# Input projections of a two-layer diffusion step: one store for both halves of a result, three buffers for latent keys and values, and the first modulation in columns of 256

## The chip, the core and the metric

The kernel runs on one core of one Trainium2 chip. The metric is device time in microseconds (us), the median of several executions. PE is the matmul engine (PEld its weight loads), DVE the vector engine, ACT the scalar engine, POOL GpSimd, SP the sync engine, whose queue issues nearly all DMAs here.

## What is computed

Two layers, each a token mixer (three groups of attention heads) and a gated convolutional feed-forward part, on 128 context tokens and 1024 latent tokens. Each token is scaled and shifted by six modulation vectors per layer, which come from two conditioning vectors. Cut to what matters here:

```python
mods = jax.nn.silu(cond) @ w_ada + b_ada
sh_m, sc_m, gt_m, sh_f, sc_f, gt_f = [m[:, None, :] for m in jnp.split(mods, 6, axis=-1)]
h = rms_norm(x, g_pre_mix) * (1 + sc_m) + sh_m
q_na, k_na, v_na, q_mla, ckv, k_rope, q_g, k_g, v_g = mixer_projections(
    h, w_in, mla_g_q, mla_w_uq, mla_g_kv, gqa_g_q, gqa_g_k)
...
o = jnp.concatenate([o_na, o_mla, o_gqa], axis=-1) @ w_out
x = x + gt_m * rms_norm(o, g_post_mix)
h = rms_norm(x, g_pre_ffn) * (1 + sc_f) + sh_f
x = x + gt_f * rms_norm(conv_ffn(h, ffn_w_up, ffn_conv_w, ffn_conv_b, ffn_w_down), g_post_ffn)
```

D_MODEL is 1024, so `w_ada` is 1024 x 6144 for each layer. The parts gt_m, sh_f and sc_f (2, 3 and 4) are first needed after the attention.

## The kernel before

The tokens are nine tiles of 128. Every layer runs in stages: `phase_a` (input projections), `phase_b` (attention), `phase_c` (output projection), `phase_u` (up projection, convolution, gate) and `Down`. Matrix products keep 32-bit accuracy by splitting each operand in a high and a low half and adding three products, so results that are read again are stored as two halves, `hi` and `lo`. `evac2` makes them from a PSUM bank: ACT writes `hi`, then DVE writes `lo = src - hi` (L205 and L206, or L208 and L209 with a scale).

`phase_a` first projects the values (V part: L374 to L376, 512 wide), then the latent heads (MLA: `mla_tile`, 416 wide, nine tiles), then the grouped heads (GQA: `gqa_tile`, nine tiles, with the pieces `mla_k` and `mla_v` spread between them), then the neighbourhood heads (NA: six groups `m` of 128 columns, L591, three chunks of 384 tokens in three PSUM banks, 72 matmuls for each group). Results go to DRAM tensors (QT, QM, KT, KM, VT, VM) by DMAs on SP's queue and are loaded again by `phase_b`. `ev` tiles hold latent keys and values on their way out, in two buffers. In the trace's names the buffers `ev2` of the NA groups also read `ev`, since trailing numbers are left out there.

Layer 0 makes its modulations 2, 3 and 4 beside this, on DVE: `ada_dve` (L297 to L324) is a generator. For each part and each stretch of `wd` columns it loads eight tiles `wadv` of 128 x `wd` (L305, two buffers) and multiplies and adds each into two accumulators `aacc`, one for each conditioning vector (L308 for the first tile, L311 for the other seven). Then PE transposes the accumulators (L320), and DVE sums the transposes (L321). It yields after each load's two instructions, and once more before the transposes: nine steps for a stretch. With `wd` = 512 there are 3 x 2 stretches, 48 loads and 54 steps.

`phase_a` advances that generator 9 + 4 times in the MLA loop, 18 times in the GQA loop and four times in each of six NA groups: 55 times in all. After the products of the last NA group, what is left of it is run to its end:

```python
if g0 and mi == 1:
    for g in ag:
        finish(g, [])
for c in range(NCH):
    sb = p.tile([128, 2, CN], F32R, name="ev2", bufs=3)
```

In layer 1 no generator runs in `phase_a`; its modulations are made in `phase_u` of layer 0 by the same function with 512 columns.

Instructions are recorded in the order in which the code makes them, and a scheduler then orders each engine's list. Each engine runs its list in order. A DMA that waits for its data or its buffer holds everything behind it on SP's queue. The first instruction of the attention on PE is a score matmul of the first latent head (L679, tile SA). The functions that the change touches:

Of the kernel before, what the change touches and what calls it, by code (L numbers as in the profile page):

```python
# [14 lines left out]
F32 = mybir.dt.float32  # L15
F32R = mybir.dt.float32r
# [15 lines left out]
CN = 384  # L32
# [13 lines left out]
def tile_kernel(ctx: ExitStack, tc: tile.TileContext, I, O):  # L46
    nc = tc.nc
# [15 lines left out]
    QT = [dram.tile([2, 12 * 64, NT], F32, name=f"QT{l}") for l in range(L)]  # L63
# [296 lines left out]
    def kcols(t):  # L360
        return (0 if t == 0 else 128) + t * 128

    def phase_a(l, z, H, w, before, rest):
# [35 lines left out]
        adst, adp = right("ad")  # L399
        ag = [ada_dve(l, z, adp, (2, 3, 4), 512)] if l == 0 else []  # L400
# [16 lines left out]
        def mla_tile(t):  # L417
# [35 lines left out]
            krT = [p.tile([32, 128], F32R, name=f"krT{e}", bufs=2) for e in range(2)]  # L453
            evac2(krT[0], krT[1], tp[0:32, 384:512])
            for e in range(2):
                nc.sync.dma_start(out=KM[l][e, :, 64:96, kc:kc + 128].rearrange("h p n -> p h n"),
                                  in_=krT[e].bitcast(F32).unsqueeze(1).to_broadcast([32, 4, 128]))
# [16 lines left out]
            qT = [p.tile([128, 4, 128], F32R, name=f"qT{e}", bufs=2) for e in range(2)]  # L474
            evac2(qT[0][0:96], qT[1][0:96], tq[0:96, :].rearrange("p (h n) -> p h n", h=4), 96.0 ** -0.5)
            for e in range(2):
                nc.sync.dma_start(out=QM[l][e, :, :, t * 128:(t + 1) * 128].rearrange("h p n -> p h n"),
                                  in_=qT[e][0:96].bitcast(F32))

        def gqa_tile(w, t):  # L480
# [22 lines left out]
            gT = [p.tile([128, 4, 128], F32R, name=f"qT{e}", bufs=2) for e in range(2)]  # L503
            evac2(gT[0], gT[1], tp.rearrange("p (h n) -> p h n", h=4))
            for e in range(2):
                nc.sync.dma_start(
                    out=QT[l][e, 384:768, t * 128:(t + 1) * 128].rearrange("(a p) n -> p a n", p=128),
                    in_=gT[e][:, 0:3].bitcast(F32))
                nc.sync.dma_start(out=KT[l][e, 384:512, kcols(t):kcols(t) + 128],
                                  in_=gT[e][:, 3].bitcast(F32))  # L510

        def mla_k(c0, n):
            for j in range(2):
# [5 lines left out]
                ks = p.tile([128, 2, 512], F32R, name="ev", bufs=2)  # L519
                evac2(ks[:, 0, :n], ks[:, 1, :n], kp[:, :n])  # L520
                for e in range(2):
                    for q in range(2):
                        nc.sync.dma_start(out=KM[l][e, 2 * j + q, 0:64, cs],
                                          in_=ks[q * 64:(q + 1) * 64, e, :n].bitcast(F32))

        def mla_v(t):
# [4 lines left out]
            vs = p.tile([128, 4, 128], F32R, name="ev", bufs=2)  # L531
# [29 lines left out]
        with tc.tile_pool(reuse_waits="tile", name="an", bufs=1) as p:  # L561
# [19 lines left out]
            for g0, ms in ((0, (0, 1, 2, 3)), (512, (4, 5))):  # L581
                whi, wlo = weights(l, wp, G_NA[0] + g0, len(ms) * 128)
                for mi, m in enumerate(ms):
# [13 lines left out]
                    for c in range(NCH):  # L597
# [3 lines left out]
                        for e in range(2):  # L601
                            sf = sb[:, e].bitcast(F32)
                            if m < 3:
                                nc.sync.dma_start(
                                    out=QT[l][e, m * 128:(m + 1) * 128, c * CN:(c + 1) * CN], in_=sf)
                            else:
                                kt = KT[l][e, (m - 3) * 128:(m - 2) * 128]
                                if c == 0:
                                    nc.sync.dma_start(out=kt[:, 0:128], in_=sf[:, 0:128])
                                    nc.sync.dma_start(out=kt[:, 256:128 + CN], in_=sf[:, 128:CN])  # L610
                                else:
                                    nc.sync.dma_start(
                                        out=kt[:, 128 + c * CN:128 + (c + 1) * CN], in_=sf)
# [804 lines left out]
```

## Time and profile before

| | |
|---|---|
| median of 3 runs | 3363.74 us (3360.38 to 3366.98) |
| the profiled execution's own time | 3362.17 us |
| its span | 3360.4 us |
| PE busy | 3205.2 us, 95% |
| DVE busy | 2169.4 us, 65% |
| ACT busy | 1544.0 us, 46% |
| POOL busy | 1124.0 us, 33% |

The span is the time from the first to the last instruction; 1.8 us of the execution's own time lie outside it. A busy time counts the engine's instructions; whether idle time of an engine costs anything is read from what waited. In the views of waits, `A <- B` says that A started when B was done. A timeline row gives start and duration in us and, in brackets, how long the engine was idle before and what ended that.

### The profile page before, as it was taken

How to read it: one execution, taken by the hardware profiler on the slowest of the kernel's cores; microseconds unless marked ns; L12 is line 12 of the kernel's file. 1: busy time of each engine (PE TensorE's matmuls, PEld its weight loads, DVE VectorE, ACT ScalarE, POOL GpSimd, SP SyncE). 2: the span in 40 equal slices, each digit the busy share in tenths (PEclk: the TensorE clock that was granted, in tenths of full speed). 3: DMA queues.
4: the chain of work that ended last, by engine and by line, in shares of the span. 5: the costliest groups of instructions: out<-in, count | busy, mean ns of one | idle time of the engine just before them, and what ended most of it. 6: DMA issues, size and time to landing. Idle time of an engine off the chain costs nothing.

```text
span 3360.4 us, 51034 instructions
## 1 busy us (share of the span) xinstructions
PE 3205.2 (95%) x18068; PEld 2891.2 (86%) x18068; DVE 2169.4 (65%) x5367; ACT 1544.0 (46%) x3209; POOL 1124.0 (33%) x962
## 2 busy tenths in 40 slices
PE   8988999989999999999999899999899999999999
PEld 3868888877899999987788799888779999999887
DVE  5796788876788888435547728888778433333443
ACT  4321688874332222235544228888643222223443
POOL 2121345431233323344421314554312332323443
PEclk9999999999999999999999899999999999999999
DMA  7467431253244333256544563215423221123665
GB/s 243 136 184 226 132 77 46 65 165 132 85 135 128 119 122 119 79 187 191 192 139 135 150 193 84 54 46 131 161 88 101 91 69 65 67 71 116 208 204 168
DMA packets 224863, 428.78 MB, mean 128 GB/s; under 512 B 21088, under 2 KB 127456, under 8 KB 224608
## 3 DMA queue, kind: packets, MB, share of 16 engines
q1 hardware_dynamic: 223312, 424.33, 41.1%
q8 instruction: 143, 2.34, 0.3%
q10 hardware_dynamic: 1296, 1.19, 0.1%
q14 instruction: 112, 0.92, 0.1%
HBM read 324.05 MB, written 101.38 MB: 127 GB/s over the span
## 4 chain that ended last, share of the span: by engine, by line
PE 70%; DVE 14%; ACT 7%; issue 4%; DMA 3%; POOL 2%; SPq 0%; ACTq 0%; DVEq 0%; POOLq 0%
PE mm L1003 31%; PE mm L1120 15%; PE O L727 4%; PE T L709 4%; PE SA L679 4%; PE mm L968 3%; ACT P L689 3%; PE mm L591 2%; DVE PT L206 2%; ACT PT L205 2%; DVE aacc L311 2%; PE mm L376 1%; DMA wadv<-w_ada 1%; PE mm L375 1%; PE mm L374 1%
## 5 line engine op out<-in xcount | busy, mean ns | idle before, releaser
L1003 PE MATMUL mm<-hhi,wu 128*128 128x384 f32 x4224 | 863.2, 335 | 2.4 <-POOL wu L200 1.6
L1003 PEld LDWEIGHTS mm<-hhi,wu 128*128 128x128 f32 x4224 | 742.7, 188 | 3.7 <-POOL wu L200 2.2
L1015 DVE SCALAR_TENSOR_TENSOR acc<-mm,conv,acc 128x336 f32<-128x336 f32 (+6 forms) x1408 | 412.7, 375 | 312.5 <-ACT acc L1040 312.3
L200 POOL TENSOR_TENSOR wu<-wraw,wu 128x1024 fp32r<-128x1024 f32 x123 | 301.2, 2451 | 683.9 <-ACT wu L197 680.4
L1003 PE MATMUL mm<-hlo,wu 128*128 128x384 f32 x2112 | 490.8, 334 | 0.0
L197 ACT CAST wu<-wraw 128x1024 fp32r<-128x1024 f32 x158 | 165.7, 1050 | 593.1 <-issue 362.2
L1003 PEld LDWEIGHTS mm<-hlo,wu 128*128 128x128 f32 x2112 | 377.2, 188 | 0.5 <-DVE hlo L153 0.3
L727 PE MATMUL O<-PT,V 128*128 128x256 f32 (+1 forms) x1936 | 334.2, 299 | 22.3 <-DVE Y L734 10.5
L698 POOL TENSOR_SCALAR P<-P,rs 128x1152 f32<-128x1152 f32 (+3 forms) x288 | 272.1, 946 | 186.2 <-DVE rs L697 120.9
L709 PE MATMUL T<-ident,P 128*128 128x128 f32 x1832 | 293.1, 278 | 16.1 <-DVE PT L206 11.8
L311 DVE SCALAR_TENSOR_TENSOR aacc<-wadv,sc,aacc 128x512 f32<-128x512 f32 x280 | 263.0, 983 | 65.2 <-DMA wadv<-w_ada 64.6
L206 DVE TENSOR_TENSOR PT<-T,PT 128x512 fp32r<-128x512 f32 (+1 forms) x448 | 284.3, 649 | 23.9 <-ACT PT L205 18.6
L727 PEld LDWEIGHTS O<-PT,V 128*128 128x128 f32 x1936 | 263.1, 192 | 39.8 <-ACT PT L205 16.6
L1120 PE MATMUL mm<-wd,g 128*128 128x512 f32 x1224 | 288.2, 392 | 2.6 <-DVE wt L166 2.6
L679 PE MATMUL SA<-k,q 128*128 128x256 f32 (+5 forms) x1224 | 282.5, 352 | 8.4 <-DVE ev L206 3.3
L1120 PEld LDWEIGHTS mm<-wd,g 128*128 128x128 f32 x1224 | 230.2, 189 | 51.4 <-DVE wt L166 3.5
L1120 PE MATMUL mm<-wu,g 128*128 128x512 f32 x1152 | 270.9, 391 | 2.6 <-DVE wt L166 2.6
L205 ACT CAST PT<-T 128x512 fp32r<-128x512 f32 (+1 forms) x448 | 241.6, 562 | 58.4 <-PE T L709 46.3
L1120 PEld LDWEIGHTS mm<-wu,g 128*128 128x128 f32 x1152 | 216.4, 188 | 48.4 <-DVE wt L166 3.5
L709 PEld LDWEIGHTS T<-ident,P 128*128 128x128 f32 x1832 | 210.4, 141 | 49.9 <-issue 17.3
L679 PEld LDWEIGHTS SA<-k,q 128*128 128x128 f32 (+1 forms) x1224 | 198.1, 192 | 32.1 <-ACT P L689 6.8
L702 DVE TENSOR_REDUCE mx<-SA 128x1 f32<-128x896 f32 (+1 forms) x192 | 182.3, 949 | 34.3 <-PE SA L679 34.3
(203 smaller groups left out, 5024.3 us busy)
## 6 DMA issues: line engine op xcount, KB each, us to landing
wraw<-w_down SPq DMA_DIRECT2D x132, 512.0 KB, 3.6
wraw<-w_up SPq DMA_DIRECT2D x88, 512.0 KB, 3.6
wadv<-w_ada SPq DMA_DIRECT2D x160, 256.0 KB, 2.8
GT<-acc SPq DMA_DIRECT2D x44, 576.0 KB, 2.8
graw<-GT SPq DMA_DIRECT2D x132, 192.0 KB, 3.1
k<-KT SPq DMA_DIRECT2D x64, 320.0 KB, 6.3
q<-QT SPq DMA_DIRECT2D x48, 288.0 KB, 6.9
XD<-xt SPq DMA_DIRECT2D x27, 512.0 KB, 2.6
```

Of the source, the lines that this page charges most:

```text
L200: (lo_eng or pool).tensor_tensor(out=lo, in0=raw, in1=hi.bitcast(F32), op=ALU.subtract)
L205: act.copy(hi, src)
L206: dve.tensor_tensor(out=lo, in0=src, in1=hi.bitcast(F32), op=ALU.subtract)
L311: dve.scalar_tensor_tensor(out=accs[i], in0=w, scalar=sc[:, k, i:i + 1], in1=accs[i], op0=ALU.mult, op1=ALU.add)
L679: pe.matmul(out, q[0:rows, qc:qc + 128], kview(k[0:rows]), start=(i == 0), stop=(i == len(passes) - 1))
L698: pool.tensor_scalar(out=P[:, :n], in0=P[:, :n], scalar1=rs, scalar2=1.0, op0=ALU.mult, op1=ALU.mult)
L702: dve.tensor_reduce(out=out, in_=src, op=ALU.max, axis=AX.X, negate=True)
L709: pe.transpose(tp[:, j * 128:(j + 1) * 128], p, ident)
L727: pe.matmul(op[0][:, c0:c1], V[:, vt, :], PT[e][:, sl, c0:c1], start=(i == 0 and e == 0), stop=(i == last and e == 1))
L1003: pe.matmul(pts[c][:, :CN], a[:, k, :], h_[:, k, c * CN:(c + 1) * CN], start=(k == 0 and a is whi and h_ is hhi), stop=(k == KC - 1 and a ...
L1015: dve.scalar_tensor_tensor(out=d, in0=src, scalar=w, in1=d, op0=ALU.mult, op1=ALU.add)
L1120: pe.matmul(pts[j], a[:, ts], d[:, 0, j * 512:(j + 1) * 512], start=(f == 0 and n == 0), stop=(f == NFF - 1 and n == 2))
```

## The change

Four things are changed, all in `phase_a`:

- The two halves of a result that were separate tiles (`krT`, `qT`, `gT`) become one tile with an axis for the half, and most stores send both halves in one DMA: QM, KT and KM from the latent and grouped heads, QT and KT from the NA groups. Over both layers 204 stores become 102. The stores of `krT` (36) and those of the grouped queries (36) stay as they are.
- `ev` has three buffers in place of two.
- In layer 0 the modulations 2, 3 and 4 are made in stretches of 256 columns: 12 stretches, 96 loads of 128 KB, 108 steps. The places at which the generator is advanced stay 55.
- `aacc` and `wadv` get half as large.

```diff
-        ag = [ada_dve(l, z, adp, (2, 3, 4), 512)] if l == 0 else []
+        ag = [ada_dve(l, z, adp, (2, 3, 4), 256)] if l == 0 else []
...
-            krT = [p.tile([32, 128], F32R, name=f"krT{e}", bufs=2) for e in range(2)]
-            evac2(krT[0], krT[1], tp[0:32, 384:512])
+            krT = p.tile([32, 2, 128], F32R, name="krT", bufs=2)
+            evac2(krT[:, 0], krT[:, 1], tp[0:32, 384:512])
...
-            qT = [p.tile([128, 4, 128], F32R, name=f"qT{e}", bufs=2) for e in range(2)]
-            evac2(qT[0][0:96], qT[1][0:96], tq[0:96, :].rearrange("p (h n) -> p h n", h=4), 96.0 ** -0.5)
-            for e in range(2):
-                nc.sync.dma_start(out=QM[l][e, :, :, t * 128:(t + 1) * 128].rearrange("h p n -> p h n"),
-                                  in_=qT[e][0:96].bitcast(F32))
+            qT = p.tile([128, 2, 4, 128], F32R, name="qT", bufs=2)
+            evac2(qT[0:96, 0], qT[0:96, 1], tq[0:96, :].rearrange("p (h n) -> p h n", h=4), 96.0 ** -0.5)
+            nc.sync.dma_start(out=QM[l][:, :, :, t * 128:(t + 1) * 128].rearrange("e h p n -> p e h n"),
+                              in_=qT[0:96].bitcast(F32))
...
-                nc.sync.dma_start(out=KT[l][e, 384:512, kcols(t):kcols(t) + 128],
-                                  in_=gT[e][:, 3].bitcast(F32))
+                    in_=gT[:, e, 0:3].bitcast(F32))
+            nc.sync.dma_start(out=KT[l][:, 384:512, kcols(t):kcols(t) + 128].rearrange("e p n -> p e n"),
+                              in_=gT[:, :, 3].bitcast(F32))
...
-                ks = p.tile([128, 2, 512], F32R, name="ev", bufs=2)
+                ks = p.tile([128, 2, 512], F32R, name="ev", bufs=3)
                 evac2(ks[:, 0, :n], ks[:, 1, :n], kp[:, :n])
-                for e in range(2):
-                    for q in range(2):
-                        nc.sync.dma_start(out=KM[l][e, 2 * j + q, 0:64, cs],
-                                          in_=ks[q * 64:(q + 1) * 64, e, :n].bitcast(F32))
+                for q in range(2):
+                    nc.sync.dma_start(out=KM[l][:, 2 * j + q, 0:64, cs].rearrange("e p n -> p e n"),
+                                      in_=ks[q * 64:(q + 1) * 64, :, :n].bitcast(F32))
...
-            vs = p.tile([128, 4, 128], F32R, name="ev", bufs=2)
+            vs = p.tile([128, 4, 128], F32R, name="ev", bufs=3)
...
-                        for e in range(2):
-                            sf = sb[:, e].bitcast(F32)
-                            if m < 3:
-                                nc.sync.dma_start(
-                                    out=QT[l][e, m * 128:(m + 1) * 128, c * CN:(c + 1) * CN], in_=sf)
+                        sf = sb.bitcast(F32)
+                        if m < 3:
+                            nc.sync.dma_start(out=QT[l][:, m * 128:(m + 1) * 128, c * CN:(c + 1) * CN].rearrange(
+                                "e p n -> p e n"), in_=sf)
+                        else:
+                            kt = KT[l][:, (m - 3) * 128:(m - 2) * 128].rearrange("e p n -> p e n")
+                            if c == 0:
+                                nc.sync.dma_start(out=kt[:, :, 0:128], in_=sf[:, :, 0:128])
+                                nc.sync.dma_start(out=kt[:, :, 256:128 + CN], in_=sf[:, :, 128:CN])
                             else:
...
+                                nc.sync.dma_start(out=kt[:, :, 128 + c * CN:128 + (c + 1) * CN], in_=sf)
```

What this does to the order shows on PE at the end of layer 0's input projections. L591 (L589 in the changed file) are the products of the last NA group, L320 the transposes of the accumulators, L679 (L675) the first scores of the attention; the numbers tell buffers apart. Before:

```order
L591 MATMUL mm<-hhi,w_3306 128x384 x3
L591 MATMUL mm<-hhi,w_3305 128x384 x3
L591 MATMUL mm<-hlo,w_3305 128x384
L320 MATMUL aux<-ident,aacc_3220 128x128 x4
L591 MATMUL mm<-hlo,w_3305 128x384 x2
L320 MATMUL aux<-ident,aacc_3221 128x128 x4
L591 MATMUL mm<-hhi,w_3306 128x384 x3
L679 MATMUL SA<-k_3570,q_3572 128x512
```

After:

```order
L589 MATMUL mm<-hhi,w_3216 128x384 x3
L320 MATMUL aux<-ident,aacc_3402 128x128 x2
L320 MATMUL aux<-ident,aacc_3403 128x128 x2
L320 MATMUL aux<-ident,aacc_3464 128x128 x2
L320 MATMUL aux<-ident,aacc_3465 128x128 x2
L320 MATMUL aux<-ident,aacc_3508 128x128 x2
L320 MATMUL aux<-ident,aacc_3509 128x128 x2
...
L320 MATMUL aux<-ident,aacc_3640 128x128 x2
L320 MATMUL aux<-ident,aacc_3641 128x128 x2
L675 MATMUL SA<-k_3732,q_3734 128x512
```

Before, the last stretch's transposes stood among the last products. After, the transposes of six stretches stand between the last product and the first score.

On SP's queue at the same place, from the stores of the last NA group (`nak` is an output) to the loads of the second latent head. Before:

```order
L305 DMA wadv<-w_ada 128x512 x2
L658 DMA k_3630<-KM_82 96x1280
L609 DMA KT_80<-ev_3520 128x128
L610 DMA KT_80<-ev_3520 128x256
L609 DMA KT_80<-ev_3520 128x128
L610 DMA KT_80<-ev_3520 128x256
L617 DMA nak<-ko 128x128
L612 DMA KT_80<-ev_3530 128x384 x2
L612 DMA KT_80<-ev_3535 128x384 x2
L661 DMA q_3632<-QM_78 96x1152
```

After:

```order
L305 DMA wadv<-w_ada 128x256 x2
L606 DMA KT_80<-ev_3686 128x2x128
L607 DMA KT_80<-ev_3686 128x2x256
L305 DMA wadv<-w_ada 128x256 x2
L613 DMA nak<-ko 128x128
L609 DMA KT_80<-ev_3694 128x2x384
L609 DMA KT_80<-ev_3698 128x2x384
L305 DMA wadv<-w_ada 128x256 x2
L664 DMA bias<-b_na 128x1280
L305 DMA wadv<-w_ada 128x256 x2
L664 DMA bias<-b_na 128x1280
L305 DMA wadv<-w_ada 128x256 x38
```

Before, no `wadv` load stood behind the last group's stores. After, 44 loads do (2 + 2 + 2 + 38), two loads of `bias` among them, and the second head's first load comes next.

## Rows read from the trace of the kernel before

**Rows 1.** The page: busy times, and the chain that ended last.

```profile
PE 3205.2 (95%) x18068; PEld 2891.2 (86%) x18068; DVE 2169.4 (65%) x5367; ACT 1544.0 (46%) x3209; POOL 1124.0 (33%) x962
...
PE 70%; DVE 14%; ACT 7%; issue 4%; DMA 3%; POOL 2%; SPq 0%; ACTq 0%; DVEq 0%; POOLq 0%
```

**Rows 2.** Stretches: MLA and GQA, then NA, of layer 0 and of layer 1.

```profile
core 0: us, PE busy (x) PEld busy (x) DVE busy (x) ACT busy (x) POOL busy (x), PEclk, DMA share, GB/s
109.00:253.00 144.00, 126.66 (x656) 109.73 (x655) 126.67 (x405) 47.90 (x130) 30.70 (x19) 0.98 0.58 161
253.00:346.00 93.00, 82.03 (x471) 78.17 (x469) 61.63 (x117) 16.42 (x36) 16.74 (x15) 1.00 0.74 224
1780.00:1910.00 130.00, 121.20 (x631) 108.36 (x629) 98.17 (x358) 46.66 (x129) 29.37 (x20) 0.97 0.46 125
1910.00:2000.00 90.00, 80.13 (x444) 78.76 (x444) 28.01 (x59) 15.79 (x35) 13.84 (x11) 0.92 0.60 178
```

**Rows 3.** Groups of DVE by shape, 108 to 346 us: count, busy us, mean ns, idle before.

```profile
L311 DVE SCALAR_TENSOR_TENSOR aacc<-wadv,sc,aacc 128x512 f32<-128x512 f32 x75 | 58.4, 799 | 17.3 <-DMA wadv<-w_ada 17.2
...
L430 DVE SCALAR_TENSOR_TENSOR cn<-mm,nw_u,gtok 128x256 f32<-128x256 f32 x9 | 4.3, 477 | 0.3
...
L432 DVE SCALAR_TENSOR_TENSOR cn<-mm,nw_u,gtok 128x128 f32<-128x128 f32 x9 | 3.0, 338 | 0.0
```

**Rows 4.** Timeline of PE, end of layer 0's projections, start of the attention.

```profile
344.07 0.60 PE L320 MATMUL aux<-ident,aacc 128*128 128x128 f32 x4
344.43 0.77 PE L591 MATMUL mm<-hhi,w 128*128 128x384 f32 x3
347.14 1.12 PE L679 MATMUL SA<-k,q 96*128 96x512 f32 x4 [1.94 <-DVE ev L206]
```

**Rows 5.** Timeline of DVE inside the NA groups of layer 0.

```profile
306.75 2.73 DVE L311 SCALAR_TENSOR_TENSOR aacc<-wadv,sc,aacc 128x512 f32<-128x512 f32 x4
...
311.63 1.42 DVE L311 SCALAR_TENSOR_TENSOR aacc<-wadv,sc,aacc 128x512 f32<-128x512 f32 x2 [1.69 <-DMA wadv<-w_ada]
...
314.90 1.41 DVE L311 SCALAR_TENSOR_TENSOR aacc<-wadv,sc,aacc 128x512 f32<-128x512 f32 x2 [1.24 <-DMA wadv<-w_ada]
```

**Rows 6.** Timeline of SP's queue, the same stretch: start and length of the issue.

```profile
308.18 0.33 SPq L305 DMA_DIRECT2D wadv<-w_ada  x1
...
313.07 0.33 SPq L305 DMA_DIRECT2D wadv<-w_ada  x1
316.35 0.33 SPq L305 DMA_DIRECT2D wadv<-w_ada  x1
```

**Rows 7.** DMA issues of the whole span: count, size, median us from issue to landing.

```profile
wadv<-w_ada SPq DMA_DIRECT2D x160, 256.0 KB, 2.8
...
bias<-b_na SPq DMA_DIRECT2D x12, 640.0 KB, 5.6
```

**Rows 8.** The same, issues of 100 to 350 us.

```profile
wadv<-w_ada SPq DMA_DIRECT2D x44, 256.0 KB, 3.3
...
wraw<-c_ckv SPq DMA_DIRECT2D x1, 64.0 KB, 1.7
```

**Rows 9.** Timeline of PE after its longest wait in the GQA stretch.

```profile
245.39 1.12 PE L320 MATMUL aux<-ident,aacc 128*128 128x128 f32 x4 [4.94 <-DVE qT L206]
...
246.73 0.63 PE L375 MATMUL mm<-w,hhi 128*128 128x512 f32 x1
```

**Rows 10.** Stretches: five us after that wait, and half a us later on.

```profile
245.40:250.40 5.00, 5.00 (x14) 4.14 (x15) 4.54 (x14) 1.04 (x1) 1.46 (x1) 0.50 0.80 223
251.50:252.00 0.50, 0.50 (x3) 0.33 (x3) 0.50 (x1) 0.00 (x0) 0.50 (x1) 1.00 0.10 37
```

**Rows 11.** Waits by releaser, 109 to 346 us: us in total, times, longest.

```profile
ACT ev L205 <- DMA VM<-ev: 13.8, 3, 8.0
...
ACT ev L208 <- DMA QT<-ev: 6.6, 3, 5.7
```

**Rows 12.** The same, 1780 to 2001 us.

```profile
ACT ev L205 <- DMA VM<-ev: 13.3, 3, 8.6
```

More of the change, by code (lines that the diff above doesn't have):

```diff
@@ L452, in mla_tile @@
             evac2(ckvT[0][:, kc:kc + 128], ckvT[1][:, kc:kc + 128], tp[:, 256:384])
-            krT = [p.tile([32, 128], F32R, name=f"krT{e}", bufs=2) for e in range(2)]
-            evac2(krT[0], krT[1], tp[0:32, 384:512])
+            krT = p.tile([32, 2, 128], F32R, name="krT", bufs=2)
+            evac2(krT[:, 0], krT[:, 1], tp[0:32, 384:512])
             for e in range(2):
                 nc.sync.dma_start(out=KM[l][e, :, 64:96, kc:kc + 128].rearrange("h p n -> p h n"),
-                                  in_=krT[e].bitcast(F32).unsqueeze(1).to_broadcast([32, 4, 128]))
+                                  in_=krT[:, e].bitcast(F32).unsqueeze(1).to_broadcast([32, 4, 128]))
             yield
@@ L502, in gqa_tile @@
                 pe.transpose(tp[:, i * 128:(i + 1) * 128], xn[:, 2 * i:2 * i + 2, :], ident)
-            gT = [p.tile([128, 4, 128], F32R, name=f"qT{e}", bufs=2) for e in range(2)]
-            evac2(gT[0], gT[1], tp.rearrange("p (h n) -> p h n", h=4))
+            gT = p.tile([128, 2, 4, 128], F32R, name="qT", bufs=2)
+            evac2(gT[:, 0], gT[:, 1], tp.rearrange("p (h n) -> p h n", h=4))
             for e in range(2):
@@ L600, in phase_a @@
                         evac2(sb[:, 0], sb[:, 1], src, 0.125 if m < 3 else None)
-                        for e in range(2):
-                            sf = sb[:, e].bitcast(F32)
-                            if m < 3:
-                                nc.sync.dma_start(
-                                    out=QT[l][e, m * 128:(m + 1) * 128, c * CN:(c + 1) * CN], in_=sf)
-                            else:
[L607 to L613, printed above, removed]
+                        sf = sb.bitcast(F32)
[7 more added lines that the diff above has]
+                                nc.sync.dma_start(out=kt[:, :, 256:128 + CN], in_=sf[:, :, 128:CN])
+                            else:
+                                nc.sync.dma_start(out=kt[:, :, 128 + c * CN:128 + (c + 1) * CN], in_=sf)
                         if m >= 3 and c == 0:
```

1 line of the change is left out of this document (removed).

## Prediction

> **What bounds the kernel now.** Start with the page. PE is busy for 95% of the span and holds 70% of the chain that ended last; DVE is second with 14% [rows 1]. So I look for changes in what PE waits for, and only in the stages that the change touches. The stretches of the input projections show how PE stands there [rows 2]. In layer 0, PE idles for 17.3 us of the 144 us of MLA and GQA and for 11.0 us of the 93 us of NA. In layer 1, which has no modulations beside its projections, it idles for 8.8 us of 130 and 9.9 us of 90. DVE is nearly as busy as PE in layer 0's MLA and GQA stretch, 126.7 us of 144, and clearly less in layer 1, 98.2 us of 130. Hence modulation work on DVE costs PE something there, at most the difference of the two layers: 14 us in MLA and GQA, 3 us in NA.
>
> Then read the end of layer 0's projections. PE finishes its last product at 344.43 + 0.77 = 345.20 us and starts the first score at 347.14 us, after waiting 1.94 us for DVE's last `lo` half [rows 4]. The last modulation transposes stand before that product, so the modulations are done when the products are. This small gap is the place to watch.
>
> **Part 1: the modulations no longer fit into the steps they are given.** With 512 columns there are 54 steps, and the loops give 55. With 256 columns there are 108 steps, and the loops still give 55: 49 of 96 loads. The other 47 are made by the code that finishes the generator, which stands after the last NA products. The order of the changed kernel confirms it: on PE, twelve groups of transposes stand between the last product and the first score, and on SP 44 loads stand behind the first store of the last NA group. That store needs the last product. So 44 loads and their DVE work can't begin before PE has run out of products, and PE, which runs its list in order, can't start the attention before the last of them is multiplied, added and transposed. Nothing covers this: ACT, POOL and PE have only attention work left, and that sits behind the transposes.
>
> What does one load cost there? The buffers are two, so a load is issued when the older buffer is free. The trace of before shows this cycle undisturbed: DVE's pair of instructions ends at 311.63 + 1.42 = 313.05 us and again at 314.90 + 1.41 = 316.31 us [rows 5], and SP issues the next loads at 313.07 and 316.35 us [rows 6], 0.02 to 0.04 us later. The load issued at 308.18 us is consumed from 311.63 us on, 3.45 us later. The cycle of one buffer is therefore landing plus DVE pair plus about 0.1 us, and two loads pass in each cycle as long as landing is longer than a DVE pair.
>
> DVE's pair at 256 columns: the trace has no such instruction from the accumulators, but L430 has the same operation and shape, 477 ns, and L432 shows 338 ns at 128 columns [rows 3]. Four at 512 columns take 2.73 us from first start to last end and two take 1.42 us [rows 5], so one adds 0.66 us where its own time is some 0.75: it overlaps the one before by about 0.08. Two at 256 columns take 0.48 + 0.40 = 0.88 us.
>
> What this shows of short instructions: 799 ns at 512 columns against 477 at 256 [rows 3], so half the columns cost 60% of the time. The Trainium skill, page "VectorE: DVE Perf Modes", section on the TRN2 errata, says that each such instruction pays a fixed latency, that for this reason tiles should have at least 512 elements, and it gives 58 cycles plus one for each element at 0.96 GHz. By that formula 256 columns would be an estimated 0.33 us, two of them about 0.65 us, and the sum below some 5 us lower; the direction speaks against this change, and I keep to the row, which is longer.
>
> Landing at 128 KB: no load of this size is in the trace. Bounds from the nearest rows: 64 KB landed in 1.7 us and 256 KB in a median of 2.8 us over the span, 3.3 us in this stretch beside other traffic [rows 7, 8]. A straight line between 64 and 256 KB gives 1.7 + (64 / 192) x 1.1 = 2.07, so 2.1 us; little else is on the queues then. The cycle is 2.1 + 0.88 + 0.08 = 3.06 us for two loads (2.66 with 1.7 us landing, 3.76 with 2.8).
>
> The tail: 44 / 2 = 22 cycles x 3.06 = 67.3 us (58.5 to 82.7). To it come: 2.0 us until the first of the 44 is issued (ACT's and DVE's evacuation of the first chunk, then one DVE pair); 3.0 us for the two `bias` loads of 640 KB that lie between them on SP and land in 5.6 us where a 256 KB load lands in 2.8 [rows 7], taken as half of that excess, 1.4, for each, rounded up; 1.5 us at the end for the last transposes and the DVE sums, whose banks the attention reuses. The transposes of a stretch's end are hidden by the next stretch's loads, which are in flight by then. From the total, 73.8 us, the old gap of 1.94 goes off: +71.9 us.
>
> **Part 2: PE's clock.** In the GQA stretch PE waited 4.94 us. Then a 512-wide matmul took 0.63 us [rows 9] and the granted clock was 0.50 for five us, which is the 1.2 GHz level, before it read 1.00, 2.4 GHz, again [rows 10]. Five us at half speed lose 2.5 us. After a wait of 70 us the attention will start at the lower level too; its first tasks wait for ACT and DVE anyway, so +2 us (0 to 3).
>
> **Part 3: less modulation work inside the products of layer 0.** Half the loads and adds leave these stretches. I give back half of the 17 us by which layer 0 is slower there: -8 us (0 to -17).
>
> **Part 4: merged stores and the third `ev` buffer, both layers.** 102 issues leave SP at some 0.33 us each [rows 6], while 48 more `wadv` issues come. SP is not on PE's path here, so that alone is worth nothing. ACT's waits for stores to free `ev` are 13.8 and 6.6 us in layer 0 and 13.3 us in layer 1 [rows 11, 12]; a third buffer removes part of the first and the last, but PE's idle time in layer 1 is 18.7 us in all [rows 2], from many causes. A merged store starts only when DVE has the `lo` half, half a us after `hi`, which keeps its buffer longer. I take -3 us (-10 to +5).
>
> **Moved loads.** The second latent head's k, q and V are behind the 44 loads on SP. They issue when the first score starts, as they did before, with the whole first head ahead of them; nothing for that.
>
> **The sum.** 3362.2 (the profiled execution; the median of the runs is 1.6 above it) + 71.9 + 2 - 8 - 3 = 3425.1, so 3426.7 against the median. Slower by 1.9%.
>
> **The rivals.**
>
> *Loads land in half the time* because they are half as large: 1.4 us, a cycle of 2.36, a tail of 52 us, 3411. Against it: 64 KB already took 1.7 us. Chance 0.09.
>
> *Loads stay as slow as whole ones*, 2.8 us: a tail of 82.7 us, 3442. For it: the landings of 3.3 us in this stretch; against it: that traffic is gone in the tail. Chance 0.12.
>
> *The stores were what held the evacuations.* All of ACT's waits for stores, 13.8 + 6.6 + 13.3 = 33.7 us, come back on PE instead of the 3 us: 3396. Against it: PE's list shows waits for DVE at the place where ACT waited longest. By the page "DMA: Bandwidth & Descriptors" of the Trainium skill (sections "Anatomy of one DMA", which gives a fixed part of about 2 us to each transfer of the GpSimd path, and "Bandwidth", which asks for larger batches) merging points in this direction. No row shows PE waiting for a store. Chance 0.05.
>
> *Not slower: DVE was the bound of the projections, and returns more than the tail takes.* All idle time of PE in the four stretches, 17.3 + 11.0 + 8.8 + 9.9 = 47 us, is returned, and the tail runs at DVE's own pace, 44 x 0.8 = 35 us, with the same 4.6 us around it: 3362 - 47 + 40 = 3355, 3356 against the median. It decides for a tail shorter than what is returned, under one us for each load, which would need landings of 1 us. Chance 0.03.
>
> **How the numbers follow.** The forecast has 0.71: 3427, with its own range of 3405 to 3447 from the bounds of landing and of parts 2 to 4. The first two rivals lie inside or at its edge. 3402 to 3447 leaves out the last two rivals and the far corners of the bounds, some 0.15. A difference of 0.2%, 6.7 us, is about what can be told from none. Slower by more: 0.96; within: 0.02; faster: 0.02, the last rival and what I don't see.
>
> **What would show it.** In the trace after: a stretch of about 70 us between the last product of layer 0 and the first score, with DVE in pairs of 0.9 us that wait for `wadv`, SP issuing nothing but `wadv`, and 24 transposes alone on PE; from that score on, times that are shifted and otherwise as before. Landing of `wadv` at 128 KB: near 2.1 us. Layer 0's first 236 us of projections shorter by about 8 us, layer 1's by a few. Wrong would be: products beside that tail, a landing far from 2.1, or a change of layer 1 by more than 10 us.

## The result, and the profile after

| | before | after |
|---|---|---|
| median | 3365.05 us (3360.38 to 3366.98, 4 runs) | 3423.48 us (3419.79 to 3426.78, 4 runs) |
| ratio | 1 | 1.0175, 95% interval 1.0163 to 1.0187 |
| the profiled execution's own time | 3362.17 us | 3422.98 us |
| its span | 3360.4 us | 3421.2 us |

The change makes the kernel slower by 1.75%, 58 us. The forecast was 3427 us, slower. The span of the profiled execution is 60.8 us longer, against 62.9 in the sum of the prediction.

The page after: PE and DVE, in 40 slices of the span (85.5 us each, busy tenths), and the granted clock of PE in the same slices.

```profile
PE 3204.7 (94%) x18068; PEld 2891.2 (85%) x18068; DVE 2184.8 (64%) x5481; ACT 1544.0 (45%) x3209; POOL 1125.8 (33%) x962
...
PE   8988299998999999999999989999899999999999
...
DVE  5785688887787788635545737888867533334343
...
PEclk9999599999999999999999999999999999999999
```

PE is busy for as long as before, within 0.5 us [rows 1]; its longer span is idle time. One digit tells where: in the fifth slice, 342 to 428 us, PE is busy for two tenths, at a clock of five tenths, and no other slice of it reads under 8. DVE is not saturated there (6).

The timeline of PE at that place (start, length, idle time before and what ended it), which answers to [rows 4]:

```profile
337.23 0.68 PE L589 MATMUL mm<-hhi,w 128*128 128x384 f32 x3
348.01 1.09 PE L320 MATMUL aux<-ident,aacc 128*128 128x128 f32 x4 [10.10 <-DVE aacc L311]
361.03 1.09 PE L320 MATMUL aux<-ident,aacc 128*128 128x128 f32 x4 [11.93 <-DVE aacc L311]
373.27 1.08 PE L320 MATMUL aux<-ident,aacc 128*128 128x128 f32 x4 [11.15 <-DVE aacc L311]
385.53 1.09 PE L320 MATMUL aux<-ident,aacc 128*128 128x128 f32 x4 [11.18 <-DVE aacc L311]
397.88 1.09 PE L320 MATMUL aux<-ident,aacc 128*128 128x128 f32 x4 [11.26 <-DVE aacc L311]
410.44 1.08 PE L320 MATMUL aux<-ident,aacc 128*128 128x128 f32 x4 [11.48 <-DVE aacc L311]
411.18 2.59 PE L675 MATMUL SA<-k,q 96*128 96x512 f32 x6
```

The last product of layer 0 ends at 337.23 + 0.68 = 337.91 us, the first score starts at 411.18: 73.27 us, in which PE has 24 transposes and nothing else. Each of the six groups of four waits 10 to 12 us for the accumulators.

What the accumulators wait for is seen on DVE, in the same stretch, which answers to [rows 5]:

```profile
353.35 1.67 DVE L311 SCALAR_TENSOR_TENSOR aacc<-wadv,sc,aacc 128x256 f32<-128x256 f32 x4 [1.90 <-DMA wadv<-w_ada]
356.47 1.75 DVE L311 SCALAR_TENSOR_TENSOR aacc<-wadv,sc,aacc 128x256 f32<-128x256 f32 x4 [1.45 <-DMA wadv<-w_ada]
359.50 1.77 DVE L311 SCALAR_TENSOR_TENSOR aacc<-wadv,sc,aacc 128x256 f32<-128x256 f32 x4 [1.28 <-DMA wadv<-w_ada]
```

Four instructions of L311 are two loads. The lots start 3.12 and 3.03 us apart, and DVE waits for `wadv` before each. SP's queue there, which answers to [rows 6], and the landing of the loads from the DMA view of 337 to 412 us (count, size, median us):

```profile
339.75 0.94 SPq L305 DMA_DIRECT2D wadv<-w_ada  x2
...
350.57 57.16 SPq L305 DMA_DIRECT2D wadv<-w_ada  x38
408.08 0.33 SPq L654 DMA_DIRECT2D k<-KM  x1
```

```profile
wadv<-w_ada SPq DMA_DIRECT2D x45, 128.0 KB, 2.1
bias<-b_na SPq DMA_DIRECT2D x2, 640.0 KB, 4.7
```

The last 38 issues of `wadv` are spread over 57.16 us, 3.01 us for two; SP holds each until a buffer is free. The stretches, which answer to [rows 2]: MLA and GQA, NA, the tail, and the two of layer 1.

```profile
109.00:250.00 141.00, 125.69 (x645) 110.76 (x644) 116.84 (x409) 48.18 (x131) 33.31 (x21) 0.96 0.52 143
250.00:338.00 88.00, 79.47 (x460) 77.02 (x458) 48.63 (x113) 15.36 (x34) 13.10 (x13) 1.00 0.71 211
338.00:411.00 73.00, 5.99 (x23) 3.54 (x24) 44.53 (x110) 2.35 (x5) 0.29 (x1) 0.53 0.41 122
1843.40:1973.40 130.00, 121.40 (x631) 108.34 (x629) 97.72 (x358) 46.64 (x129) 30.70 (x20) 0.97 0.46 127
1973.40:2062.00 88.60, 80.36 (x443) 79.31 (x444) 26.68 (x58) 14.60 (x32) 12.48 (x10) 0.92 0.58 177
```

Layer 0's projections are shorter (141 and 88 us for the 144 and 93 of before), the tail is new, and layer 1 is nearly as it was: 130 and 88.6 us for 130 and 90.

**The time followed through the program.** Four places are found in both timelines. MLA of layer 0 starts at 108.92 us before and 109.15 after. The first score starts at 347.14 and 411.18: 64.04 us later. MLA of layer 1 starts at 1780.02 and 1843.40: 63.38 later. Layer 1's first score starts at 2000.73 and 2062.20: 61.47 later. The end is 60.8 later. So the whole loss arises before the first score, and 1.9 us less are spent in layer 1's projections.

### The profile page after: what moved, and what is told of

The parts are those of the page before. It is cut to its first block, busy times and chain, and to the rows that moved or that the text cites. A ratio compares the mean times of both kernels' runs of the same rounds, so it can differ in the third digit from the quotient of the medians.

```text
span 3421.2 us, 51133 instructions
## 1 busy us (share of the span) xinstructions
PE 3204.7 (94%) x18068; PEld 2891.2 (85%) x18068; DVE 2184.8 (64%) x5481; ACT 1544.0 (45%) x3209; POOL 1125.8 (33%) x962
## 4 chain that ended last, share of the span: by engine, by line
PE 61%; DVE 8%; ACT 4%; issue 2%; POOL 1%; DMA 1%; SPq 0%; DVEq 0%; ACTq 0%; POOLq 0%
PE mm L999 31%; PE mm L1116 14%; PE mm L964 3%; PE O L723 2%; PE mm L589 2%; PE T L705 2%; PE SA L675 2%; ACT P L685 1%; DVE nw_t L116 1%; PE mm L375 1%; PE mm L376 1%; PE mm L374 1%; DVE PT L206 1%; ACT PT L205 1%; PE aux L148 1%
## 5 line engine op out<-in xcount | busy, mean ns | idle before, releaser
L311 DVE SCALAR_TENSOR_TENSOR aacc<-wadv,sc,aacc 128x512 f32<-128x512 f32 (+1 forms) x364 | 279.8, 815 | 88.9 <-DMA wadv<-w_ada 88.3
L675 PE MATMUL SA<-k,q 128*128 128x256 f32 (+5 forms) x1224 | 280.4, 350 | 5.2 <-ACT P L685 2.8
L675 PEld LDWEIGHTS SA<-k,q 128*128 128x128 f32 (+1 forms) x1224 | 196.5, 190 | 28.2 <-ACT P L685 7.1
```

Of the source, the lines that this page charges most:

```text
L311: dve.scalar_tensor_tensor(out=accs[i], in0=w, scalar=sc[:, k, i:i + 1], in1=accs[i], op0=ALU.mult, op1=ALU.add)
L675: pe.matmul(out, q[0:rows, qc:qc + 128], kview(k[0:rows]), start=(i == 0), stop=(i == len(passes) - 1))
```

## The experiments

**Theory.** The generator gets 55 advances and needs 108; what is left over stands behind the last product, where two buffers and small loads set the pace. **Rivals**: another part of the change costs the time; the pace in the tail is DVE's own; more advances alone are the remedy. Each ratio is against the kernel before on the same chip.

### Which part does it

Only the columns, in the kernel before:

```diff
-        ag = [ada_dve(l, z, adp, (2, 3, 4), 512)] if l == 0 else []
+        ag = [ada_dve(l, z, adp, (2, 3, 4), 256)] if l == 0 else []
```

> The kernel before with one edit: the first modulation in columns of 256 (stores and ev buffers as before). Theory (the tail of 44 loads is all of the slowdown, merged stores and the third buffer are worth -2 to -4 us): before plus the new gap of 73.3 us in front of the first score, less the old one of 1.9 and less about 7 that the products of layer 0 give back: 3365 + 64 = 3429 us, 3424 to 3434. Rival (merged stores hold things up and make a good part of the slowdown): 3395 or less. Second rival (merged stores gain much, 10 us or more, and hide part of the loss): 3434 and above.

Measured: 3427.82 us (3426.75 to 3430.33), ratio 1.0190 (1.0176 to 1.0204). PE's timeline has the same six groups of transposes, from 350.27 to 413.92 us; the last product ends at 340.91 and the first score starts at 414.66, 73.75 us later. The time is in the expected range, and both rivals (3395 or less, 3434 and above) fall.

Only the merged stores, in the changed kernel (the `ev` buffers go back with the columns, since this kernel's tiles don't fit in the memory on the chip with 512 columns and three `ev` buffers):

```diff
-        ag = [ada_dve(l, z, adp, (2, 3, 4), 256)] if l == 0 else []
+        ag = [ada_dve(l, z, adp, (2, 3, 4), 512)] if l == 0 else []
...
-                ks = p.tile([128, 2, 512], F32R, name="ev", bufs=3)
+                ks = p.tile([128, 2, 512], F32R, name="ev", bufs=2)
...
-            vs = p.tile([128, 4, 128], F32R, name="ev", bufs=3)
+            vs = p.tile([128, 4, 128], F32R, name="ev", bufs=2)
```

> The changed kernel with columns of 512 again and ev in two buffers (512 columns and three ev buffers don't fit in memory together): so only the merged stores are left of the change. Theory: no load stands behind the last product; 3365 less 2 to 4 us: 3362, 3358 to 3366. Rival (the merging makes part of the slowdown): 3380 or above. Rival (stores were what held the evacuations): 3350 or below.

Measured: 3361.98 us (3359.70 to 3370.05), ratio 0.9996 (0.9988 to 1.0005): in the expected range, and not told from no change. So the columns carry the whole loss, and 102 fewer DMA issues carry nothing that can be measured.

### What sets the pace of the tail

The changed kernel with two `ev` buffers, and four `wadv` buffers in place of two:

```diff
-                    w = p.tile([128, wd], F32, name="wadv", bufs=2)
+                    w = p.tile([128, wd], F32, name="wadv", bufs=4 if wd == 256 else 2)
```

> The changed kernel with four buffers for wadv in place of two (ev goes back to two buffers to make room). The 47 loads are still behind the last product. Theory (two buffers make each pair of loads pay a landing of 2.2 us plus a DVE pair): with four, loads are in flight while DVE works, a stretch of eight loads costs 8 x 0.83 us of DVE plus 1.5 us for its transposes, 8.2 us in place of 12.4; 5.5 such stretches: 23 us less, 3400 us, 3394 to 3406. Rival (DVE's instructions set the pace of the tail): 3420 or above, as no DVE work is removed. Rival (transfers in flight share the queues, and each lands later): 3407 to 3419.

Measured: 3396.04 us (3387.87 to 3398.01), ratio 1.0088 (1.0073 to 1.0103). Some of PE's timeline, then DVE's:

```profile
362.77 1.09 PE L320 MATMUL aux<-ident,aacc 128*128 128x128 f32 x4 [6.66 <-DVE aacc L311]
370.11 1.09 PE L320 MATMUL aux<-ident,aacc 128*128 128x128 f32 x4 [6.25 <-DVE aacc L311]
378.95 1.09 PE L320 MATMUL aux<-ident,aacc 128*128 128x128 f32 x4 [7.76 <-DVE aacc L311]
379.69 2.59 PE L675 MATMUL SA<-k,q 96*128 96x512 f32 x6
```

```profile
364.73 5.62 DVE L311 SCALAR_TENSOR_TENSOR aacc<-wadv,sc,aacc 128x256 f32<-128x256 f32 x14
```

The time is in the expected range. Once the `bias` loads are through, eight loads take 7.3 to 8.8 us in place of 12.2 to 12.6 (9.2 and 13.0 in the stretch with the `bias` loads), with the same loads and sums, 47 loads of them still made by the code behind the last products. In the best of these stretches DVE runs 14 instructions with no wait, 0.40 us each. So the pace of two buffers was the wait for landing, and DVE's own pace is the next limit, some 7 us for eight loads. The tail stays, as the theory has it, and is shorter: 45.10 us from the last product (its end at 334.59) to the first score. That last product also ends 3.3 us earlier than with two buffers (337.91), so four buffers do not by themselves lengthen the products. The `ev` buffer taken back here is worth nothing that can be told, as a run below shows.

### Are more advances the remedy

The changed kernel with two advances of the generator where it had one:

```diff
             advance(ag)
+            advance(ag)
             if t % 2:
                 advance(ag)
+                advance(ag)
...
-            advance(ag)
-            advance(ag)
+            for _ in range(4):
+                advance(ag)
...
-                        if k % 2 == 0:
-                            advance(ag)
+                        advance(ag)
```

> The changed kernel with twice as many advances of the modulations in each loop (110 in place of 55, for 108 steps), so that their 96 loads are placed beside the products; all else as in the changed kernel. Theory (what costs is the place of the loads, not their number): the tail goes but for a few us at the end; twice as many short DVE instructions cost layer 0's projections up to 8 us over the kernel before; merging gives back 2 to 4: 3366 us, 3360 to 3374. Rival (96 short loads cost as much wherever they stand, since DVE waits for each): 3385 or above.

Measured: 3382.89 us (3382.12 to 3384.33), ratio 1.0056 (1.0043 to 1.0068). The expectation missed: the time lies between its range and the rival's. PE at the end of layer 0's projections, then SP:

```profile
346.99 0.68 PE L590 MATMUL mm<-hhi,w 128*128 128x384 f32 x3
356.24 1.08 PE L320 MATMUL aux<-ident,aacc 128*128 128x128 f32 x4 [8.57 <-DVE aacc L311]
370.47 1.08 PE L320 MATMUL aux<-ident,aacc 128*128 128x128 f32 x4 [13.15 <-DVE aacc L311]
```

```profile
348.50 0.38 SPq L607 DMA_DIRECT2D KT<-ev  x1
...
349.50 0.44 SPq L305 DMA_DIRECT2D wadv<-w_ada  x1
...
352.87 2.46 SPq L305 DMA_DIRECT2D wadv<-w_ada  x2
...
358.24 9.70 SPq L305 DMA_DIRECT2D wadv<-w_ada  x6
```

Two of the twelve stretches of columns still stand behind the last product, with eleven loads behind the last group's first store (some of them in rows left out). The 72 products of an NA group take PE 12.5 us (24 times 0.52, the time from 346.47 to 346.99 us for three of them), and each group is now given eight advances, some seven loads, since nine advances make eight loads and their transposes. Through two buffers eight loads take 12.2 us or more with DVE free, so seven take an estimated 10.7, and that leaves little room. Where a group's evacuations lie between, two lots of two loads start 5.2 us apart in place of 3.1:

```profile
332.89 1.68 DVE L311 SCALAR_TENSOR_TENSOR aacc<-wadv,sc,aacc 128x256 f32<-128x256 f32 x4 [1.81 <-DMA wadv<-w_ada]
334.48 1.49 DVE L206 TENSOR_TENSOR ev<-mm,ev 128x384 fp32r<-128x384 f32 x3
338.09 1.68 DVE L311 SCALAR_TENSOR_TENSOR aacc<-wadv,sc,aacc 128x256 f32<-128x256 f32 x4 [2.12 <-DMA wadv<-w_ada]
```

So the loads seem to fall behind the products. If that is the cause, four buffers on top must remove the rest of the tail. If the number of buffers does not matter, they must not:

```diff
-                    w = p.tile([128, wd], F32, name="wadv", bufs=2)
+                    w = p.tile([128, wd], F32, name="wadv", bufs=4 if wd == 256 else 2)
```

> The changed kernel with two advances of the generator wherever it had one (as in the run with doubled advances, 3382.89 us) and with four wadv buffers in place of two; ev has two buffers again, for want of memory. Theory, pace: with two buffers eight loads took 12.2 to 12.6 us, as long as one NA group's products with their evacuations, so the doubled advances could not keep up and two stretches of transposes were left behind the last product. With four buffers eight loads took 7.3 to 8.8 us, so now they keep up: no stretch behind the last product, first score within 3 us of it. Sum: 3362 for merged stores alone, +2.5 for the products of layer 0, which ended at 347.67 instead of 345.20 us with doubled short instructions: 3364.5 (3359 to 3371). Rival, place: the loads that stand behind stores on SP, or a lack of DVE time, left those stretches, and the number of buffers does not matter: 3378 or more.

Measured: 3371.53 us (3364.41 to 3373.82), ratio 1.0021 (1.0012 to 1.0031). PE's timeline:

```profile
353.78 0.80 PE L320 MATMUL aux<-ident,aacc 128*128 128x128 f32 x4 [0.90 <-DVE aacc L311]
354.34 0.77 PE L590 MATMUL mm<-hhi,w 128*128 128x384 f32 x3
354.95 0.68 PE L590 MATMUL mm<-hlo,w 128*128 128x384 f32 x3
355.48 0.68 PE L590 MATMUL mm<-hhi,w 128*128 128x384 f32 x3
357.36 1.50 PE L676 MATMUL SA<-k,q 96*128 96x512 f32 x6 [1.20 <-ACT ko L613]
```

The last transposes stand before the last products again and the score starts 1.20 us after them: the tail is gone, and the number of `wadv` buffers did it (two `ev` buffers alone leave the tail, as the next run shows). Here no `wadv` load stands behind the last group's stores on SP either, so the pace of the loads and their place changed together, and these runs don't tell the two apart. The last product ends at 356.16 us, 10.96 us later than before [rows 4] and 8.8 later than with merged stores alone (347.34), against the 2.5 that I had put into the sum. So the time is 7 us over the expected one and just above its range, and the kernel is still slower than before. The groups of DVE by shape, 90 to 412 us, first before, then this kernel, show what DVE pays (busy us, mean ns):

```profile
L311 DVE SCALAR_TENSOR_TENSOR aacc<-wadv,sc,aacc 128x512 f32<-128x512 f32 x84 | 64.7, 793 | 21.4 <-DMA wadv<-w_ada 21.2
L308 DVE TENSOR_SCALAR aacc<-wadv,sc 128x512 f32<-128x512 f32 x12 | 5.7, 478 | 0.0
```

```profile
L311 DVE SCALAR_TENSOR_TENSOR aacc<-wadv,sc,aacc 128x256 f32<-128x256 f32 x168 | 79.3, 506 | 11.0 <-DMA wadv<-w_ada 10.8
L308 DVE TENSOR_SCALAR aacc<-wadv,sc 128x256 f32<-128x256 f32 x24 | 8.1, 344 | 0.1
```

The same modulations take DVE 87.4 us in columns of 256 and 70.4 in columns of 512: 17.0 us more on the engine whose evacuations PE waits for. How that reaches PE is seen between the start of MLA and the last product: 246.88 us here, 236.28 before, 237.17 with merged stores alone. Of the 9.7 us over merged stores alone, PE idles 6.3 (30.4 against 24.1; its waits for DVE are 29.7 against 22.9). The other 3.4 are busy time for the same work, at granted clocks of 0.92 (MLA and GQA) and 0.95 (NA) against 0.95 and 0.96. Over the kernel before, idle time is only 2.9 of the 10.6 us and busy time 7.7 (granted clock 0.98 and 1.00 there). That the short instructions on DVE cause all of this is argued from these sums; no run changes them alone.

### What the third `ev` buffer is worth

The kernel with doubled advances and two `ev` buffers, against the same with three (3382.89 us):

```diff
-                ks = p.tile([128, 2, 512], F32R, name="ev", bufs=3)
+                ks = p.tile([128, 2, 512], F32R, name="ev", bufs=2)
...
-            vs = p.tile([128, 4, 128], F32R, name="ev", bufs=3)
+            vs = p.tile([128, 4, 128], F32R, name="ev", bufs=2)
```

> The run with doubled advances (3382.89 us), with two ev buffers in place of three and nothing else changed: what the third buffer is worth. Theory: PE does not wait for stores, so the third buffer is worth nothing that can be told: 3383 (3379 to 3387). Rival: ACT's waits for stores hold the products; a third of its 33.7 us or more comes back as loss: 3390 or more.

Measured: 3384.54 us (3384.41 to 3389.83), ratio 1.0068 (1.0054 to 1.0081), against 1.0056 (1.0043 to 1.0068) with three. The time is in the expected range, and the two intervals overlap: nothing that can be told is lost with the buffer. The tail is there in the same form, with the first score at 371.56 us (371.21 with three).

### What the modulations cost beside products

The generator of layer 0's parts 2 to 4 is left out and its results are set to zero, so its 96 loads, sums and transposes are not done:

```diff
-        ag = [ada_dve(l, z, adp, (2, 3, 4), 256)] if l == 0 else []
+        ag = []
+        if l == 0:
+            for part in (2, 3, 4):
+                pool.memset(z.mods[:, part], 0.0)
+                ada_done(z, part)
```

> The changed kernel with the whole generator of layer 0's parts 2 to 4 left out: its 96 loads, its sums and its transposes are not done and the three parts are set to zero, so the output differs; all the rest is as in the changed kernel. It prices the modulation work where it stands beside products. Theory: half of it gave 7.3 us back (last product of layer 0 at 337.91 instead of 345.20 us), so all of it gives some 15: 3362 - 15 = 3347 (3341 to 3353), layer 0's last product near 331. Rival, the stretches are held by loads of weights, stores and evacuations as layer 1 is, and the first half was all that there was to gain: 3354 or more.

Measured: 3345.41 us (3343.26 to 3346.96), ratio 0.9947 (0.9933 to 0.9960). Layer 0's last product:

```profile
328.65 0.68 PE L593 MATMUL mm<-hhi,w 128*128 128x384 f32 x3
```

It ends at 329.33 us, and the time is in the expected range. Against that, the end of the products prices the modulations as they stand beside them: 15.9 us for all of them in columns of 512 (345.20, before; 18.0 with merged stores alone, 347.34), 8.6 us for 49 of 96 loads in columns of 256 (337.91, after), 5.3 for 49 with four buffers (334.59), 26.8 us for all 96 with four buffers (356.16). These ends also hold what differs ahead of MLA, whose first product starts between 108.75 us (here) and 110.17 (merged stores alone); counted from that start, 15.9 and 18.0 become 15.7 and 16.6. With four buffers 96 loads cost far more than twice what 49 do, so the price is not one for each load. Moving half of the work behind the products gave 7.3 us back and left 73.3 us there, where 1.9 were before.

### Two tries for a kernel that is faster than both

The second accumulator made by ACT and POOL, which have room, in place of DVE (512 columns, merged stores, two `ev` buffers):

```diff
                     for i in range(2):
-                        if k == 0:
+                        if l == 0 and i == 1:
+                            act.mul(accs[1] if k == 0 else w, w, sc[:, k, 1:2])
+                            if k > 0:
+                                pool.tensor_tensor(out=accs[1], in0=w, in1=accs[1], op=ALU.add)
+                        elif k == 0:
```

> Merged stores, 512 columns, two ev buffers (3361.98 us so far), and the second accumulator of layer 0's generator made by ACT (multiply, in place) and POOL (add) in place of DVE. Theory: DVE's share of the modulations is what costs the products of layer 0 their some 15 us; half of it leaves DVE, ACT and POOL have room there (48 and 31 us busy of 144), so about half comes back: 3355 (3348 to 3361). Rival: a load is held longer (landing, DVE, ACT, POOL one after the other, some 2.8 + 0.75 + 0.6 + 1.3 us, for two buffers 2.7 us a load), and the evacuations of ACT and the rotations of POOL queue behind those waits: 3366 or more.

Measured: 3387.20 us (3382.36 to 3388.43), ratio 1.0068 (1.0055 to 1.0081). The expectation missed, and the rival's time came. Its waits, 109 to 372 us (us in total, times, longest):

```profile
POOL aacc L310 <- ACT wadv L308: 111.0, 23, 33.4
ACT wadv L308 <- DVE aacc L315: 42.4, 21, 5.5
DVE aacc L315 <- DMA wadv<-w_ada: 32.1, 13, 4.8
```

The chain of a load now goes over three engines with two buffers. ACT, which makes the `hi` halves, waits 42.4 us for DVE to be done with a load, and DVE waits 32.1 us for the next load (12.0 in the kernel it is made from, in the same stretch). POOL's 111.0 us are mostly idle time of an engine with little else to do there; PE waits for POOL's sums for 1.5 us in all. The last product ends at 371.83 us, 24.5 later than in that kernel, though half of DVE's modulation work is gone. From the start of MLA, PE idles 17.1 us more and is busy 7.8 us longer for the same work, at granted clocks of 0.93 and 0.90. The work taken off DVE came back as waits, in two in-order lists.

The second advance of a tile in the GQA loop behind that tile's other pieces:

```diff
             g = gqa_tile(w2, t)
             next(g)
             advance(gens)
             advance(ag)
-            advance(ag)
             gens.append(g)
             for u in units[13 * t // NTT:13 * (t + 1) // NTT]:
                 u()
+            advance(ag)
```

> Merged stores, 512 columns, two ev buffers (3361.98 us), and in the GQA loop the second of the two advances of a tile stands behind that tile's pieces of latent keys and values in place of right behind the first. A try for a kernel that is faster than both. Theory: in the run it is made from, DVE waits 16.1 us in 13 waits for wadv, and what stands behind it on DVE's list is evacuations that PE waits for; two loads that are asked for at once and land in 3.2 us make such waits, and spreading them takes some of the waits away: 3359 (3355 to 3363). Rival: these waits are covered by PE's products in progress, or the pieces' evacuations queue behind the additions instead: 3362 to 3368, no difference that can be told.

Measured: 3361.06 us (3357.62 to 3367.10), ratio 0.9992 (0.9983 to 1.0001): not told from no change. DVE's waits for `wadv` in layer 0 are 18.7 us in 12 waits, where the kernel it is made from has 16.1 in 13; so the edit didn't do what it was for. The median lies inside the expected range, but the mechanism expected is not there, and the rival's "no difference that can be told" is what the run shows. No kernel of this study that computes the same result is measurably faster than the kernel before.

## Why the prediction was right

| step | predicted, us | measured, us |
|---|---|---|
| last product to first score | 73.8 | 73.27 |
| cycle of two loads | 3.06 | 3.03 to 3.12 |
| landing of 128 KB | 2.1 | 2.1 in the tail, 2.2 over layer 0 |
| DVE pair at 256 columns | 0.88 | 0.88 |
| loads behind the last product | 44 | 44 |
| half clock at the attention's start | +2 | hidden in a difference of -0.7 against before; +2.0 against merged stores alone |
| products of layer 0 | -8 | -7.3 |
| merged stores, third buffer | -3 | not told from 0; -1.9 in layer 1 is not theirs |
| difference of the spans | +62.9 | +60.8 |

**The tail** was right in its place, its count and its pace, and the tail decides the forecast. Two sizes in it were not quite right. The `bias` loads were put at 3.0 us. From the first of the 44 loads at 339.75 to the 38 from 350.57 on, six loads and both `bias` loads took 10.82 us, which is 1.6 more than three cycles of 3.06. And eight loads take 12.24 to 12.56 us from one group of transposes to the next, up to 0.3 more than four cycles; with the end of the tail that adds 1.0 us over the 38 loads. These two misses nearly offset each other, so that the tail came out within 0.5 us is partly luck. The range, too, is narrower than the working: the bounds that the prediction names add up to 3400 and 3459, and its lower end is given once as 3405 and once as 3402.

**Which row set the landing.** The straight line between 64 KB (1.7 us) and 256 KB [rows 7, 8] gave 2.1, and 2.1 was measured. The rival of loads that land in half the time (1.4 us) falls by the measured landing, and so does the one of 2.8 us. That the wait for landing, not DVE's work, sets the pace is shown by four buffers, which make the cycle shorter with only the third `ev` buffer taken back beside them.

**The price of a short instruction** was rightly taken from a row of this kernel [rows 3], 477 ns at 256 columns; L311 has a median of 479 ns. The prediction doesn't say that L430 reads a PSUM bank (`mm`) where L311 reads a loaded tile; that the two agree was not known beforehand. By the Trainium skill's page "VectorE: DVE Perf Modes", section on the TRN2 errata, it would be an estimated 0.33 us by the table's 58 cycles, which is too short here; the same section says that the table comes out too low for single instructions, and its formula for float32 additions, (N + 151) / 0.96 ns, gives an estimated 0.42. The Trainium skill's direction there, that short instructions pay a fixed part each, is what the trace shows: in the run with doubled advances and four buffers the same sums take DVE 17 us more.

**The clock** can't be read from the difference of the two kernels. PE did fall to half speed in the tail: the granted clock reads 0.53 in that stretch, and the first score takes 2.59 us where it took 1.48. Yet from the first score to layer 1's projections the kernel after takes 1432.22 us, 0.66 less than the kernel before. The kernel before had scores at half speed just behind its own start:

```profile
354.20 2.59 PE L679 MATMUL SA<-k,q 96*128 96x512 f32 x6
...
357.72 2.59 PE L679 MATMUL SA<-k,q 96*128 96x512 f32 x6
```

After, PE is back at full speed by its second set of scores (1.38 us at 414.01) and shows no score of 2.59 in the ten us behind that. But a tail does not simply move that slow stretch. In the four other kernels with a tail (columns alone, four buffers, and the two with doubled advances and two `wadv` buffers) the first score takes 2.59 us and scores of 2.40 to 2.59 come again eight to nine us later. With four buffers, whose first score starts at 379.69:

```profile
388.33 2.59 PE L675 MATMUL SA<-k,q 96*128 96x512 f32 x6
...
391.85 2.59 PE L675 MATMUL SA<-k,q 96*128 96x512 f32 x6
```

Of the kernels with merged stores, the five without a tail take 1429.7 to 1430.4 us from the first score to layer 1's projections (1430.24 with merged stores alone), the four with one 1432.2 to 1434.2. By these traces, one of each kernel, some 2 to 4 us go with a tail, and the +2 is about right in size; that the clock is all of it is not shown. The difference of before and after hides it, since merged stores alone are 2.6 us shorter there than the kernel before (1432.88). Part of that 2.6 is the clock again (two sets of scores of 2.14 and 1.87 us where before has 2.59 twice); what makes the rest stays open.

**The products of layer 0** gave 7.3 us for 8 predicted. The run without the modulations shows 15.9 to 18.0 us for all of them, on both sides of the 17 that the comparison of the layers gave. That half of the work costs half of it holds with two buffers (8.6 us); with four it doesn't (5.3 for 49 loads, 26.8 for 96).

**Stores and buffers.** ACT's waits for `VM` stores fell from 13.8 to 7.9 us in layer 0 and from 13.3 to 5.8 in layer 1 [rows 11, 12], and PE returned nothing that can be told. In layer 1 the third buffer did this, not the merging: two buffers show 12.2 us with merged stores alone and 13.2 with doubled advances, three show 5.8 after and 6.2 with doubled advances. The waits of layer 0 and of layer 1 after:

```profile
ACT ev L205 <- DMA VM<-ev: 7.9, 2, 4.6
```

```profile
ACT ev L205 <- DMA VM<-ev: 5.8, 2, 4.4
```

The rival that these waits were PE's falls: taking the third buffer away again costs nothing that can be told. Nor are the 1.9 us of layer 1 the stores' or the buffer's. From the start of layer 1's MLA to its first score the kernel before takes 220.71 us and the one after 218.80, but the kernel with the columns alone, which has neither edit, takes 218.37, and merged stores alone 220.47. What makes these two us stays open. So no run shows the -3 us of this step, though its range (-10 to +5) holds what was measured; that it lies near the 1.9 us of layer 1 is luck.

**The rival that DVE was the bound** fell with its condition: it needed a tail under the time that is returned, and 73.3 us stand against 9.2 (7.3 + 1.9) that were saved elsewhere.

## What to carry to other kernels

A generator that is advanced a fixed number of times beside other work has a hidden contract: its number of steps must fit the number of advances. Halving its step size halves what is hidden, and the rest runs alone, here at the pace of a load's landing and use divided by the buffers. Before giving such work more steps, compare the cycle of its loads (landing + use, over the number of buffers) with the time between two advances, and count what the shorter instructions add on the engine that carries them. Not tried here: parts 2 to 4 are first needed after the attention, so what is left of the generator might be advanced beside the attention instead of being run to its end before it.

## What was not expected of the hardware

A load of half the size landed in 2.1 us where 256 KB take a median of 2.8, as the prediction's straight line has it; what is easily overlooked is what that does to a stream: for the same 512 KB through two buffers that is 2 x (2.1 + 0.88 + 0.08) = 6.1 us against an estimated 2.8 + 1.42 + 0.08 = 4.3 us, from the rows on landing and on DVE's instructions [rows 5, 7]. Four loads in flight instead of two didn't slow each other in the tail: 2.2 us against 2.1 for 128 KB. Beside the products they landed later: a median of 2.7 us over all 96 loads with doubled advances and four buffers, 2.3 with two.

Removing 102 of 204 stores, and with them 102 issues on SP, moved the time by no more than 0.12% (0.9988 to 1.0005), though SP's queue carries nearly all transfers.
